# A decoder block's feed-forward part: gate and up projections by block products in Strassen's manner, the hidden values through DRAM

## The chip, the cores and the metric

One core of one Trainium2 chip runs the whole program in one launch. The metric is device time in microseconds (us), the median of three timed runs; a profiled execution beside them gives the trace. The engines that compute are TensorE (PE; its weight loads are listed as PEld), VectorE (DVE), ScalarE (ACT) and GpSimd (POOL). SyncE (SP) issues the DMAs; its queue is SPq.

## The reference

One decoder layer over 1024 tokens of width 1024, all float32: a norm and one combined input projection; eight heads of dilated sliding-window attention and eight heads of RWKV-7 time mixing; one output projection with a residual; then a norm and a SwiGLU feed-forward part of width 2816 (`D_FF`). The change lies in that last part:

```python
    x = x + mixed @ w_out
    xn2 = rms_norm(x, norm2_g).astype(x.dtype)
    ffn = (jax.nn.silu(xn2 @ w_gate) * (xn2 @ w_up)) @ w_down
    return x + ffn
```

## The kernel before, in words

**Precision.** A float32 product is made of three passes. Each operand is split (`split`): a rounded copy `hi` that ACT writes (fp32r) and a remainder `lo` that DVE or POOL forms as source minus `hi`. The passes are hi x hi, hi x lo and lo x hi, summed in PSUM (`passes`, `mm3`).

**Order of work.** The program is written as generators ("streams"), each with a rank. A planner (`Flow`) steps through them with modelled costs and times and emits every instruction in the order in which its model would start it; among those that are ready the lower rank goes first. `Wait`, `Mark`, `Get` and `Free` order the streams in the model and hand out PSUM banks. On the chip each engine then executes its own list strictly in that order, and waits at an instruction until the data it needs is there. SP issues its DMAs in order too.

**The feed-forward part.** It comes last, after attention, time mixing and the output projection (`outproj`, sums into `acc`, eight tiles of 128 tokens x 1024).
- `norms2` norms a tile of 128 tokens: ACT squares and sums, two small POOL steps give the factor, DVE multiplies by factor and gain (tile `nxn`), PE transposes eight blocks into two banks, and ACT and DVE split them into `x2h` and `x2l`. Two streams work on the first four tiles, then two on the last four. `xnh[h]`, `xnl[h]` hold token half h (512 tokens).
- `load_weights` brings 128 columns of gate or up (512 KB, unit u) into `ffraw`, ACT and DVE split them into `ffhi` and `fflo`. Units alternate gate, up, over 22 rows of 128 features (`NFF`).
- `ffproj` (PE): for each unit and token half 24 matmuls of 128x128 weights against 128x512 tokens: eight blocks of the inner dimension, three passes. The first two units are run on half 0 first, then on half 1.
- `hidden`: ACT takes the gate product from its bank through silu, DVE multiplies by the up product, ACT and DVE split the result into `hh` and `hl`, which stay in SBUF.
- `load_down` brings 128 rows of `w_down` and splits them; `down` takes two feature rows at a time (`GS`): for eight token tiles and two column halves six matmuls into one of two banks, 16 sums in all, and `accumulate` (DVE) adds each sum to `acc`. After the last group the tiles of `acc` are written out.

So projection and down projection alternate on PE, group by group. Eight PSUM banks are free in this part (`bank0` to `bank3`, `chain0`, `chain1`, `mm0`, `mm1`).

## Time and profile before

| | |
|---|---|
| timed runs | median 1536.94 us (1536.3 to 1537.02, three runs) |
| profiled execution | 1528.85 us, of it 1527.1 us span from the first to the last instruction |
| instructions in the trace | 23747 |
| DMA | 137.07 MB, mean 90 GB/s |
| HBM | 105.10 MB read, 26.21 MB written |
| chain that ended last | PE 57% of the span, DMA 3%, DVE 2% |

The page gives the busy time of each engine and its share of the span. PE's records of two neighbouring matmuls overlap (their ends are modelled), so the distance from start to start is what one costs. The chain is followed back from the last instruction, at each step to what released it. A group of instructions is one line: engine, operation, output<-inputs by the program's names, shapes, count, busy time, mean ns of one, idle time of the engine just before them and what ended it.

### The profile page before, as it was taken

How to read it: one execution, taken by the hardware profiler on the slowest of the kernel's cores; microseconds unless marked ns; L12 is line 12 of the kernel's file. 1: busy time of each engine (PE TensorE's matmuls, PEld its weight loads, DVE VectorE, ACT ScalarE, POOL GpSimd, SP SyncE). 2: the span in 40 equal slices, each digit the busy share in tenths (PEclk: the TensorE clock that was granted, in tenths of full speed). 3: DMA queues.
4: the chain of work that ended last, by engine and by line, in shares of the span. 5: the costliest groups of instructions: out<-in, count | busy, mean ns of one | idle time of the engine just before them, and what ended most of it. 6: DMA issues, size and time to landing. Idle time of an engine off the chain costs nothing.

```text
span 1527.1 us, 23747 instructions
## 1 busy us (share of the span) xinstructions
PE 1461.2 (96%) x8950; PEld 1181.5 (77%) x8950; DVE 774.6 (51%) x1705; ACT 610.3 (40%) x1546; POOL 340.5 (22%) x416
## 2 busy tenths in 40 slices
PE   8899999999899997998999999999999999999998
PEld 6667776776777776887878888888888888888887
DVE  5466677765664365776884424334242433424333
ACT  6434655557657765666754121111211112121110
POOL 5432434335544562325420000000000000000000
PEclk9999999999999998999999999999999999999999
DMA  6342232232323349995422021020211202021102
GB/s 203 104 113 67 62 99 69 76 89 77 105 83 107 106 141 283 276 229 146 112 70 85 27 69 56 29 69 14 83 36 47 59 25 77 21 70 55 42 1 111
DMA packets 171669, 137.07 MB, mean 90 GB/s; under 512 B 35617, under 2 KB 143393, under 8 KB 171554
## 3 DMA queue, kind: packets, MB, share of 16 engines
q1 hardware_dynamic: 171554, 135.55, 30.9%
q8 instruction: 71, 1.16, 0.3%
q14 instruction: 44, 0.36, 0.1%
HBM read 105.10 MB, written 26.21 MB: 86 GB/s over the span
## 4 chain that ended last, share of the span: by engine, by line
PE 57%; DMA 3%; DVE 2%; issue 1%; SPq 1%; ACT 1%; POOL 1%; POOLq 0%; ACTq 0%; DVEq 0%
PE bank L227 28%; PE chain L227 15%; PE mm L227 13%; DMA kk<-kl_d 1%; SPq L227 1%; DMA qv<-ql_d 0%; DMA kk<-kh_d 0%; DMA mixr<-mix_d 0%; DMA woraw<-in_w_out_dram 0%; ACT nxn L227 0%; DMA bias<-in_tab_dram 0%; DVE acc L227 0%; DVE ml L227 0%; ACT mh L227 0%; POOL nrs L227 0%
## 5 line engine op out<-in xcount | busy, mean ns | idle before, releaser
L227 ACT ACTIVATE dh<-wdraw 128x1024 fp32r<-128x1024 f32 x22 | 23.3, 1061 | 252.2 <-PE bank L227 229.1
L227 POOL TENSOR_TENSOR inlo<-inraw,inhi 128x512 fp32r<-128x512 f32 x62 | 81.6, 1320 | 110.3 <-ACT inhi L227 100.3
L227 DVE TENSOR_TENSOR acc<-chain,acc 128x512 f32<-128x512 f32 x96 | 66.4, 692 | 75.3 <-PE chain L227 75.3
L227 DVE TENSOR_TENSOR acc<-bank,acc 128x512 f32<-128x512 f32 x105 | 72.6, 691 | 62.2 <-PE bank L227 62.0
L227 DVE TENSOR_TENSOR fflo<-ffraw,ffhi 128x1024 fp32r<-128x1024 f32 x44 | 53.8, 1222 | 94.5 <-ACT ffhi L227 91.0
L227 ACT ACTIVATE hh<-sg 128x512 fp32r<-128x512 f32 x44 | 27.8, 633 | 152.9 <-DVE sg L227 152.9
L227 PE MATMUL bank<-x2l,ffhi 128*128 128x512 f32 x352 | 87.9, 389 | 0.0
L227 PE MATMUL bank<-x2h,fflo 128*128 128x512 f32 x352 | 87.5, 390 | 0.0
L227 PE MATMUL bank<-x2h,ffhi 128*128 128x512 f32 x352 | 87.1, 389 | 0.0
L227 ACT ACTIVATE ffhi<-ffraw 128x1024 fp32r<-128x1024 f32 x44 | 46.5, 1057 | 82.0 <-PE mm L227 52.9
L227 PEld LDWEIGHTS bank<-x2h,fflo 128*128 128x128 f32 x352 | 66.0, 188 | 13.8
L227 PEld LDWEIGHTS bank<-x2l,ffhi 128*128 128x128 f32 x352 | 66.1, 188 | 13.7
L227 PEld LDWEIGHTS bank<-x2h,ffhi 128*128 128x128 f32 x352 | 66.0, 188 | 13.7
L227 PE MATMUL chain<-dh,hh 128*128 128x512 f32 x176 | 68.6, 390 | 0.0
L227 PE MATMUL chain<-dl,hh 128*128 128x512 f32 x176 | 68.6, 390 | 0.0
L227 PE MATMUL chain<-dh,hl 128*128 128x512 f32 x176 | 68.5, 389 | 0.0
L227 PE MATMUL bank<-dh,hh 128*128 128x512 f32 x176 | 68.5, 389 | 0.0
L227 PE MATMUL bank<-dl,hh 128*128 128x512 f32 x176 | 68.5, 389 | 0.0
L227 PE MATMUL bank<-dh,hl 128*128 128x512 f32 x176 | 68.5, 389 | 0.0
L227 DVE TENSOR_TENSOR sg<-bank,sg 128x512 f32<-128x512 f32 x23 | 15.9, 692 | 83.0 <-PE bank L227 83.0
L227 DVE SCALAR_TENSOR_TENSOR S<-chain,ec,Sp 64x64 f32<-64x64 f32 x112 | 31.6, 282 | 51.0 <-PE chain L227 40.9
L227 PE MATMUL mm<-x2l,ffhi 128*128 128x512 f32 x224 | 55.3, 389 | 0.0
(359 smaller groups left out, 3692.9 us busy)
## 6 DMA issues: line engine op xcount, KB each, us to landing
inraw<-in_w_in_dram SPq DMA_DIRECT2D x62, 256.0 KB, 3.0
ffraw<-in_w_gate_dram SPq DMA_DIRECT2D x22, 512.0 KB, 4.7
ffraw<-in_w_up_dram SPq DMA_DIRECT2D x22, 512.0 KB, 4.9
wdraw<-in_w_down_dram SPq DMA_DIRECT2D x22, 512.0 KB, 3.5
rkv_d<-stage SPq DMA_DIRECT2D x24, 256.0 KB, 2.3
xt<-in_x_dram SPq DMA_DIRECT2D x8, 512.0 KB, 7.2
v_d<-v SPq DMA_DIRECT2D x16, 256.0 KB, 2.3
woraw<-in_w_out_dram SPq DMA_DIRECT2D x16, 256.0 KB, 4.9
```

The costliest lines, as they stand in the source:

```text
L227: op.fn(*op.a, **op.k)
```

## The change

For each feature row of 128 the gate and up weights are cut into four blocks: A11, A12 (gate, first and second half of the inner dimension), A21, A22 (up). The normed tokens are cut likewise: B11, B21 (tokens 0 to 511, both halves of the inner dimension), B12, B22 (tokens 512 to 1023). The four results, gate and up for both token halves, are made of seven block products in place of eight, in Winograd's form of Strassen's scheme: S1 = A21 + A22, S2 = S1 - A11, S3 = A11 - A21, S4 = A12 - S2, and on the token side T1 = B12 - B11, T2 = B22 - T1, T3 = B22 - B12, T4 = B21 - T2. A block product is 12 matmuls (four blocks, three passes).

- `norms2` now makes B11 and B21 of the first four tiles. `combine` norms the last four and forms B22 and T1 to T4 of them, each split in two.
- The first two feature rows (`NCL`) are made classically: four products K on the first token half, then four products L on T1 and B22, to which the partial sums kept from K are added. They use neither S nor T2 to T4.
- `fetch_ff` brings pieces of 256 KB into six raw buffers (`NFRAW`): four per feature row, later pieces of `w_down` and of h. `prepare_ff` forms S1 to S4 (POOL, DVE) and splits each operand into one of five buffers (`NOPS`); POOL makes the remainders of the unchanged blocks, DVE those of the sums.
- `ffproj` runs the products in the order P1, P6, P2, P7, P5, P4, P3. P2 adds onto P1's bank, P4 onto P7's, P3 onto P5's, each after another engine has read that bank: ACT copies P1 (`gates`), DVE forms U2 = P1 + P6, U3 = U2 + P7, C22 = U3 + P5, C21 = U2 + (P7 + P4), C12 = U2 + (P5 + P3) (`hidden`).
- The hidden values go to a DRAM tensor `h_d`, a block of 128 features x 512 tokens at a time.
- `down` starts when all products are done: for each token half eight banks collect the sums over all 22 feature rows; h and `w_down` are fetched and split again for it, `w_down` once per token half. `finals` adds each bank to `acc` once and writes it out in pieces of 256 KB.

```diff
-GS = 2
+NCL = 2
+NOPS = 5
+NFRAW = 6
...
+    h_d = dram.tile([DFF, S], F32, name="h_d")
...
-    def load_weights(pool, srcs, name, rbufs=1, sbufs=2, eng=DVE):
...
+    def combine(e):
+        for i in range(4 + e, 8, 2):
+            o = slice(128 * (i - 4), 128 * (i - 4) + 128)
+            yield Wait(("added", 1, i, 0), ("added", 1, i, 1), ("x2", 2 + e))
+            xn = T(pf, [128, D], F32, f"nxn{e}")
+            rs = T(pf, [128, 1], F32, f"nrs{e}")
+            yield from row_rsqrt(rs, T(pf, [128, 1], F32, f"nss{e}"), acc[i], xn)
+            yield DVE.scalar_tensor_tensor(out=xn, in0=acc[i], scalar=rs[:, 0:1], in1=g2bc, op0=ALU.mult, op1=ALU.mult)
+            tags = yield Get(n=2)
+            ps = [bank(t) for t in tags]
+            for q in range(2):
+                yield from transposes(ps[q], xn[:, 512 * q:512 * q + 512])
+            p12, p22 = [p.rearrange("p (k t) -> p k t", k=4) for p in ps]
+            (h11, l11), (h21, l21), (h22, l22) = [[t[:, :, o] for t in ff[x]] for x in ("B11", "B21", "B22")]
+            (h1, l1), (h2, l2), (h3, l3), (h4, l4) = [[t[:, :, o] for t in ff[x]] for x in ("T1", "T2", "T3", "T4")]
+            tt = T(pf, [128, 2, 4, 128], F32, f"tt{e}", tag=f"nxn{e}")
+            t1, t2 = tt[:, 0], tt[:, 1]
+            t3, t4 = T(pf, [128, 4, 128], F32, f"t3{e}", tag=f"sw{e + 1}"), t1
+            def less(o_, a_, b_, eng=DVE):
+                return eng.tensor_tensor(out=o_, in0=a_, in1=b_, op=ALU.subtract)
+            yield less(t1, p12, h11.bitcast(F32))
+            yield POOL.tensor_tensor(out=t1, in0=t1, in1=l11.bitcast(F32), op=ALU.subtract)
+            yield ACT.activation(h22, p22, AF.Copy)
+            yield ACT.activation(t3, p22, AF.Copy)
+            yield DVE.tensor_tensor(out=t3, in0=t3, in1=p12, op=ALU.subtract)
+            yield less(t2, p22, t1)
+            yield less(l22, p22, h22.bitcast(F32))
+            yield ACT.activation(h1, t1, AF.Copy)
+            yield ACT.activation(h3, t3, AF.Copy)
+            yield less(l1, t1, h1.bitcast(F32))
+            yield POOL.tensor_tensor(out=t4, in0=h21.bitcast(F32), in1=t2, op=ALU.subtract)
+            yield ACT.activation(h2, t2, AF.Copy)
+            yield DVE.tensor_tensor(out=t4, in0=t4, in1=l21.bitcast(F32), op=ALU.add)
+            yield less(l3, t3, h3.bitcast(F32), POOL)
+            yield less(l2, t2, h2.bitcast(F32))
+            yield ACT.activation(h4, t4, AF.Copy)
+            yield less(l4, t4, h4.bitcast(F32))
             yield Mark(("x2", i))
...
+    fraws, nop, fops = {}, [0], {}
+    corners = [(0, 0), (1, 0), (0, 1), (1, 1)]
+    pieces = [(p, r, q, "K") for p in range(NCL) for r, q in corners] + [(p, r, q, "L") for p in range(NCL) for r in range(2) for q in range(2)]
+    pieces += [(p, r, q, "S") for p in range(NCL, NFF) for r in range(2) for q in range(2)]
+    blocks2 = [(th, f, j, "down") for th in range(2) for f in range(NFF) for j in range(3)]
+    rawlist = pieces + blocks2
+    def fetch_ff():
+        for n, key in enumerate(rawlist):
+            if n >= NFRAW:
+                yield Wait(("rawfree", rawlist[n - NFRAW]))
+            raw = T(pf, [128, 4, 128], F32, "fraw", bufs=NFRAW)
+            if n < len(pieces):
+                p, r, q, _ = key
+                yield SP.dma_start(raw, wv[r][q][:, :, p * 128:(p + 1) * 128])
+            else:
+                th, f, j = key[0:3]
+                flat = raw.rearrange("p k t -> p (k t)")
+                if j == 1:
+                    yield Wait(("h", f, th))
+                    yield SP.dma_start(flat, h_d[f * 128:(f + 1) * 128, th * HB:(th + 1) * HB])
+                else:
+                    yield SP.dma_start(flat, w_down[f * 128:(f + 1) * 128, j // 2 * HB:j // 2 * HB + HB])
+            fraws[key] = raw
+            yield Mark(("raw", key))
+    def operand(key, src, eng):
+        n = nop[0]
+        nop[0] += 1
+        if n >= NOPS:
+            yield Wait(("opused", n - NOPS))
+        hi = T(pf, [128, 4, 128], F32R, "oph", bufs=NOPS)
+        lo = T(pf, [128, 4, 128], F32R, "opl", bufs=NOPS)
+        yield from split(src, hi, lo, eng)
+        fops[key] = hi, lo, n
+        yield Mark(("op", key))
+    def prepare_ff():
+        for key in pieces[0:8 * NCL]:
+            p, r, q, kind = key
+            yield Wait(("raw", key))
+            yield from operand((p, f"{kind}{r}{q}"), fraws[key], POOL)
+            yield Mark(("rawfree", key))
+        yield Wait(*[("x2", i) for i in range(4, 8)])
+        for p in range(NCL, NFF):
+            keys_ = [(p, r, q, "S") for r in range(2) for q in range(2)]
+            yield Wait(*[("raw", key) for key in keys_])
+            a11, a12, a21, a22 = [fraws[key] for key in keys_]
+            yield from operand((p, "A11"), a11, POOL)
+            s1 = fresh("sw1")
+            yield POOL.tensor_tensor(out=s1, in0=a21, in1=a22, op=ALU.add)
+            s2 = fresh("sw2")
+            yield DVE.tensor_tensor(out=s2, in0=s1, in1=a11, op=ALU.subtract)
+            yield from operand((p, "S2"), s2, DVE)
+            yield from operand((p, "A12"), a12, POOL)
+            s3 = fresh("sw3")
+            yield POOL.tensor_tensor(out=s3, in0=a11, in1=a21, op=ALU.subtract)
+            yield Mark(("rawfree", keys_[0]))
+            yield Mark(("rawfree", keys_[2]))
+            yield from operand((p, "S3"), s3, DVE)
+            yield from operand((p, "S1"), s1, DVE)
+            yield from operand((p, "A22"), a22, POOL)
+            yield Mark(("rawfree", keys_[3]))
+            s4 = fresh("sw4", "sw3")
+            yield DVE.tensor_tensor(out=s4, in0=a12, in1=s2, op=ALU.subtract)
+            yield Mark(("rawfree", keys_[1]))
+            yield from operand((p, "S4"), s4, DVE)
+        for key in blocks2:
+            yield Wait(("raw", key))
+            yield from operand(key, fraws[key], DVE)
+            yield Mark(("rawfree", key))
...
-    first = [flow.add(8.05, norms2(e, 2, 0, pf)) for e in range(2)]
-    flow.add(20, load_weights(pf, ffsrc, "ff", rbufs=2))
+    first = [flow.add(8.05, norms2(e)) for e in range(2)]
+    flow.add(20, fetch_ff())
+    flow.add(20.5, prepare_ff())
...
-    flow.add(8.05, norms2(0, 2, 1, pf))
-    flow.add(8.05, norms2(1, 2, 1, PG))
+    ff.update({x: [T(PG, [128, 4, HB], F32R, f"{x}{n}") for n in "hl"] for x in ("B22", "T1", "T2", "T3", "T4")})
+    for e in range(2):
+        flow.add(8.05, combine(e))
+    banks2 = {}
+    plan = [(p, f"{x}{j}") for x in "KL" for p in range(NCL) for j in range(1, 5)]
+    plan += [(p, x) for p in range(NCL, NFF) for x in ("P1", "P6", "P2", "P7", "P5", "P4", "P3")]
+    terms = {"K1": ("K00", "B11", "a", True, None), "K2": ("K10", "B11", "e", True, None), "K3": ("K01", "B21", "a", False, "s1"),
+             "K4": ("K11", "B21", "e", False, "q1"), "L1": ("L00", "T1", "d", True, None), "L2": ("L01", "B22", "d", False, None),
+             "L3": ("L10", "T1", "f", True, None), "L4": ("L11", "B22", "f", False, None),
+             "P1": ("A11", "B11", "a", True, None), "P2": ("A12", "B21", "a", False, "s1"), "P3": ("S4", "B22", "d", False, "C22"),
+             "P4": ("A22", "T4", "c", False, "u3"), "P5": ("S1", "T1", "d", True, None), "P6": ("S2", "T2", "b", True, None),
+             "P7": ("S3", "T3", "c", True, None)}
     def ffproj():
...
+        for p, x in plan:
+            w, b, acc_, begins, taken = terms[x]
+            yield Wait(("op", (p, w)), *[("x2", i) for i in (range(4) if b in ("B11", "B21") else range(4, 8))])
+            if taken:
+                yield Wait((taken, p))
+            if begins:
+                tag = yield Get()
+                banks2[p, acc_] = bank(tag), tag
+            ps = banks2[p, acc_][0]
+            wh, wl, n = fops[p, w]
+            i = 0
+            for a_, b_ in passes(wh, wl, *ff[b]):
+                for k in range(4):
+                    yield PE.matmul(out=ps, lhsT=a_[:, k, :], rhs=b_[:, k, :], start=(i == 0 and begins), stop=(i == 11), skip_group_check=True)
+                    i += 1
+            yield Mark(("opused", n))
+            yield Mark((x, p))
+    sg0, s1s, q1s = {}, {}, {}
+    def taken_(store, p, name):
+        store[p] = T(PG, [128, HB], F32, "first", bufs=4)
+        yield ACT.activation(store[p], banks2[p, name][0], AF.Copy)
+    def gates():
+        for p in range(NFF):
+            classical = p < NCL
+            yield Wait(("K1" if classical else "P1", p))
+            if not classical:
+                yield Wait(("h", NCL - 1, 1) if p < NCL + 4 else ("u2", p - 4))
+            yield from taken_(s1s, p, "a")
+            yield Mark(("s1", p))
...
+            yield Wait(("K3" if classical else "P2", p))
+            if p >= 2:
+                yield Wait(("h", p - 2, 0))
+            sg0[p] = T(PG, [128, HB], F32, "sg0", bufs=2)
+            yield ACT.activation(sg0[p], banks2[p, "a"][0], AF.Silu)
+            yield Free(banks2[p, "a"][1])
+            yield Mark(("sg0", p))
...
     def hidden():
...
+        def plus(o, p, name, other):
+            return DVE.tensor_tensor(out=o, in0=banks2[p, name][0], in1=other, op=ALU.add)
...
+        for p in range(NCL, NFF):
+            rows = slice(p * 128, (p + 1) * 128)
+            yield Wait(("P6", p), ("s1", p))
+            uu = T(pf, [128, 2, HB], F32, "uu", tag="nxn0")
+            u2, u3 = uu[:, 0, :], uu[:, 1, :]
+            yield plus(u2, p, "b", s1s[p])
+            yield Free(banks2[p, "b"][1])
+            yield Mark(("u2", p))
+            yield Wait(("P7", p))
+            yield plus(u3, p, "c", u2)
+            yield Mark(("u3", p))
+            yield Wait(("P5", p))
+            up1 = T(pf, [128, 2, HB], F32, "up1", tag="nxn1")
+            c22, c12 = up1[:, 0, :], up1[:, 1, :]
+            yield plus(c22, p, "d", u3)
+            yield Mark(("C22", p))
+            yield Wait(("P4", p), ("sg0", p))
+            c21 = T(pf, [128, HB], F32, "up0", tag="g2bc")
+            yield plus(c21, p, "c", u2)
+            yield Free(banks2[p, "c"][1])
+            yield POOL.tensor_tensor(out=c21, in0=c21, in1=sg0[p], op=ALU.mult)
+            yield SP.dma_start(h_d[rows, 0:HB], c21)
+            yield Mark(("h", p, 0))
+            yield Wait(("P3", p))
+            yield plus(c12, p, "d", u2)
+            yield Free(banks2[p, "d"][1])
+            yield ACT.activation(c12, c12, AF.Silu)
+            yield DVE.tensor_tensor(out=c22, in0=c22, in1=c12, op=ALU.mult)
+            yield SP.dma_start(h_d[rows, HB:S], c22)
+            yield Mark(("h", p, 1))
+    downs = {}
     def down():
...
+        yield Wait(("P3", NFF - 1))
+        for th in range(2):
+            for f in range(NFF):
+                d0, h, d1 = [(th, f, j, "down") for j in range(3)]
+                for hf, d in enumerate((d0, d1)):
+                    for i in range(4):
+                        if i == 0:
+                            yield Wait(("op", h), ("op", d))
+                        if f == 0:
+                            tag = yield Get()
+                            downs[th, i, hf] = bank(tag), tag
+                        m = 0
+                        for a_, b_ in passes(*fops[h][0:2], *fops[d][0:2]):
+                            yield PE.matmul(out=downs[th, i, hf][0], lhsT=a_[:, i, :], rhs=b_.rearrange("p k t -> p (k t)"),
+                                            start=(f == 0 and m == 0), stop=(f == NFF - 1 and m == 2), skip_group_check=True)
+                            m += 1
+                        if f == NFF - 1:
+                            yield Mark(("dsum", th, i, hf))
...
+    flow.run([flow.add(21, gates()), flow.add(22, hidden()), flow.add(22.5, finals()), flow.add(24, down()), flow.add(25, ffproj())])
```

## Rows read from the trace of the kernel before

**Rows 1.** The page, part 1: busy us, share of the span, instructions

```profile
PE 1461.2 (96%) x8950; PEld 1181.5 (77%) x8950; DVE 774.6 (51%) x1705; ACT 610.3 (40%) x1546; POOL 340.5 (22%) x416
```

**Rows 2.** Windows: engine busy us (count), clock, DMA share, GB/s

```profile
900.00:1000.00 100.00, 100.00 (x442) 82.76 (x441) 37.48 (x49) 15.18 (x19) 0.00 (x0) 1.00 0.13 37
```

**Rows 3.** PE's waits, 770 to 1527 us: total, times, longest; two of four

```profile
PE mm L227 <- DVE O L227: 1.1, 1, 1.1
...
PE bank L227 <- DVE d L227: 0.2, 1, 0.2
```

**Rows 4.** The chain of waits: start, us, what

```profile
891.36 5.44 PE bank L227 x24
```

**Rows 5.** Timeline at the part's start: start, us, what [idle before]

```profile
799.02 0.39 PE L227 MATMUL bank<-woh,ml 128*128 128x512 f32 x1
799.25 1.99 PE L227 MATMUL chain<-x2h,ffhi 128*128 128x512 f32 x8
...
799.27 0.19 ACT L227 ACTIVATION_READ_ACCUMULATOR nxn<-acc 128x1 f32 x1
799.36 1.05 ACT L227 ACTIVATE nxn<-acc 128x1024 f32<-128x1024 f32 x1
...
799.54 0.19 POOL L227 TENSOR_SCALAR nss<-nss 128x1 f32<-128x1 f32 x1 [5.81 <-ACT nxn L227]
799.82 0.54 POOL L227 TENSOR_TENSOR nrs<-nss,nhalf 128x1 f32<-128x1 f32 x1
...
800.39 1.28 DVE L227 SCALAR_TENSOR_TENSOR nxn<-acc,nrs,g2bc 128x1024 f32<-128x1024 f32 x1 [0.25 <-POOL nrs L227]
...
800.58 1.15 POOL L227 TENSOR_SCALAR nss<-nss 128x1 f32<-128x1 f32 x1 [0.23 <-ACT nxn L227]
...
802.39 1.28 DVE L227 SCALAR_TENSOR_TENSOR nxn<-acc,nrs,g2bc 128x1024 f32<-128x1024 f32 x1 [0.71 <-POOL nrs L227]
...
802.90 0.60 PE L227 MATMUL mm<-cs,nxn 128*128 128x128 f32 x4
803.25 0.94 PE L227 MATMUL chain<-x2h,fflo 128*128 128x512 f32 x3
```

**Rows 6.** Groups of instructions by form: busy us, mean ns

```profile
L227 ACT ACTIVATE hh<-sg 128x512 fp32r<-128x512 f32 x44 | 27.8, 633 | 152.9 <-DVE sg L227 152.9
...
L227 DVE TENSOR_TENSOR hl<-sg,hh 128x512 fp32r<-128x512 f32 x44 | 30.3, 689 | 16.1 <-ACT hh L227 16.1
...
L227 DVE TENSOR_TENSOR M<-bank,rc 128x512 f32<-128x512 f32 x16 | 11.1, 691 | 15.6 <-PE bank L227 15.5
...
L227 POOL TENSOR_TENSOR inlo<-inraw,inhi 128x512 fp32r<-128x512 f32 x62 | 81.6, 1320 | 110.3 <-ACT inhi L227 100.3 <-PE mm L227 6.3 <-PE chain L227 3.6
```

**Rows 7.** Timeline of DVE and POOL, 239 to 243 us

```profile
239.64 0.67 DVE L227 TENSOR_TENSOR ra<-kx,E 128x512 f32<-128x512 f32 x1
...
240.96 1.55 POOL L227 TENSOR_TENSOR inlo<-inraw,inhi 128x512 fp32r<-128x512 f32 x1 [6.09 <-ACT inhi L227]
241.28 1.78 DVE L227 TENSOR_TENSOR ra<-rx,E 128x512 f32<-128x512 f32 x1
```

**Rows 8.** Busy time by window after a starved stretch

```profile
700.00:702.00 2.00, 1.01 (x10) 0.80 (x9) 1.89 (x3) 1.17 (x4) 2.00 (x2) 1.00 0.35 121
702.00:704.00 2.00, 2.00 (x10) 1.99 (x11) 0.24 (x1) 1.32 (x6) 1.54 (x2) 0.50 0.77 230
704.00:706.00 2.00, 2.00 (x12) 1.66 (x11) 0.54 (x2) 1.57 (x4) 1.09 (x1) 0.65 0.93 253
```

**Rows 9.** The page, part 6: DMA issues, KB each, us to landing

```profile
inraw<-in_w_in_dram SPq DMA_DIRECT2D x62, 256.0 KB, 3.0
ffraw<-in_w_gate_dram SPq DMA_DIRECT2D x22, 512.0 KB, 4.7
```

**Rows 10.** PE's last instruction; busy time of the first 20 us

```profile
1522.84 0.39 PE L227 MATMUL bank<-dh,hl 128*128 128x512 f32 x1
...
0.00:20.00 20.00, 14.33 (x70) 8.21 (x71) 10.39 (x22) 11.90 (x23) 7.77 (x22) 1.00 0.89 310
```

More of the change, by code (lines that the diff above doesn't have):

```diff
@@ L1584, in accumulate @@
-    def accumulate():
-        m = 0
-        for g in range(NFF // GS):
-            for i in range(8):
-                for hf in range(2):
-                    cs_ = slice(hf * HB, (hf + 1) * HB)
-                    yield Wait(("dsum", m))
-                    yield DVE.tensor_tensor(out=acc[i][:, cs_], in0=products["down", m], in1=acc[i][:, cs_], op=ALU.add)
-                    yield Mark(("added", m))
-                    m += 1
-                    if g == NFF // GS - 1 and (hf or i == 7):
-                        cs_ = cs_ if i == 7 else slice(0, D)
-                        yield SP.dma_start(out[i * 128:(i + 1) * 128, cs_], acc[i][:, cs_])
```

131 lines of the change are left out of this document (49 added, 82 removed).

## The prediction

> **What bounds the kernel now.** I read the page's busy shares first: TensorE (PE) is busy 96% of the span, the next engine about half of it [rows 1]. A share over 1527.1 us mixes stages, so I cut the span into windows. From 800 us on, where the feed-forward part lies, a stretch of 100 us holds 100.00 us of PE at the full granted clock, while VectorE (DVE) has 37, ScalarE (ACT) 15, GpSimd (POOL) nothing and DMA an eighth [rows 2]. Then the waits of PE itself over 770 to 1527 us: the largest of four is 1.1 us, the sum 3.2 us [rows 3]. The chain of waits shows what one product costs: 24 matmuls in 5.44 us, 0.2267 us each, product after product without a gap [rows 4]. The part starts at 799.25 us, 0.23 us behind the last matmul of the output projection [rows 5], and ends near 1523 us [rows 10]. Count: 22 rows of 128 features, two projections, two token halves, 24 matmuls = 2112, and 22 x 16 x 3 = 1056 of the down projection; 3168 x 0.2267 = 718.1 us, which with the transposes fills that stretch. So PE alone bounds this half: a matmul taken away is worth 0.2267 us until something else ends last.
>
> **The change part by part.**
>
> *Matmuls.* The two classical rows keep 8 products of 12. Each of the 20 Strassen rows has 7 x 12 = 84 in place of 96: 240 fewer, of the same form (128x128 against 128x512, one weight load each). 240 x 0.2267 = **-54.4 us**. The down projection keeps its 1056.
>
> *Start.* The first product needs tokens 0 to 511 normed, as before, and that point is set by PE's own output projection [rows 5], so nothing is gained. DVE loses the two weight remainders it made there, POOL gets five of 1.32 us [rows 6], and a norm's small POOL steps can stand behind one. 0 to 1.3 us; I take **0.5**, since the wait is at most one operation and DVE is relieved.
>
> *The second token half.* Its four tiles now also yield T1 to T4, while PE has only the eight K products to do. Cover: 96 x 0.2267 = 21.8 us plus 32 transposes at 0.35 us for four (802.90 to 803.25) = 2.8 [rows 5], so K ends at 799.25 + 24.6 = 823.8. PE then needs T1 and B22 of all four tiles (T2 to T4 only later, behind 21.8 us of L products). Tiles go in pairs, since the buffer of a tile's normed rows is also that of its sums. Lower end, each step as soon as its inputs are there: from the square to the normed rows 4.3 us (799.36 to 802.39 + 1.28) [rows 5], transposes 1.0, then through T4 one after the other four DVE steps, two on POOL and an ACT copy: 4 x 0.69 + 2 x 1.32 + 0.63 and 0.9 of handovers (0.08 from 799.27 + 0.19 to 799.54 [rows 5]; I put 0.1 to 0.15 each) = 6.9 [rows 6]. Tile 5 has its normed rows at 803.67 and is through at 811.6; tile 7 then needs 4.3 + 1.0 + DVE 0.69, POOL 1.32, ACT 0.63, DVE 0.69 and 0.5 to have T1: 820.7, no stall. Upper end: POOL and DVE don't run independently. In this very place a POOL step of 0.19 us takes 1.15 while DVE works on two SBUF operands [rows 5], and a DVE operation of 0.67 us takes 1.78 beside a POOL one, ending after it [rows 7]. So I add both. Per tile: normed rows 1.28, four DVE steps with both operands in SBUF 2.76, small POOL steps 0.19 + 0.54 = 0.73, three POOL differences 3.96 = 8.7; two tiles 17.5; the other two up to T1 8.1; two more POOL steps of tile 6 2.6; six weight remainders of K and L that POOL makes meanwhile 7.9. Sum 36.1 us from 800.39: 836.5, a stall of 12.7. I take **9**, nearer the upper end, because rows 5 show the contention in the same instructions and place.
>
> The Trainium skill, page "SBUF — State Buffer", section "Who interferes with whom", says that a DVE instruction with two SBUF inputs and a GpSimd one that reads SBUF exclude each other for the whole instruction. The trace agrees (0.67 against 1.78 us). Taken strictly the rule gives the upper end here, and rival B below; without it the stall would be nil.
>
> *Clock.* After a stretch in which PE was half busy (1.01 of 2.00 us) the granted clock read 0.50 and 0.65 for two windows of 2 us [rows 8], the lower level of 1.2 GHz for most of them: 1.0 + 0.7 = 1.7 us. A stall of some us before L should cost this once: **2** (0 to 3).
>
> *One Strassen row.* PE: 84 x 0.2267 = 19.04 us. DVE: two differences, four remainders, five sums with PSUM, one product: 12 x 0.69 = 8.3. ACT: seven copies, the first sum, two silus: 10 x 0.63 = 6.3. POOL: three remainders, two sums, one product: 6 x 1.32 = 7.9. DMA: 1.5 MB per row. No engine is near 19. What can hurt is order. (a) P2 waits until ACT has taken P1 from the bank, P4 until DVE has added U3, P3 until DVE has added C22; all later products queue behind them on PE. Each has one other product, 2.72 us, between; 0.69 and a handover of 0.2 leave 1.8, more than the 1.11 that one exclusion costs [rows 7]; two in a row cost 0.4. (b) The fourth raw piece of a row is fetched only when S4 of the row before has been formed; from its landing to the next S4 stand 0.63 + 1.32 (A11), 1.32 (S1), 0.69 (S2), 0.63 + 0.63 + 1.32 (copies of S2 and A12, A12's remainder), 1.32 (S3), 0.63 and three DVE steps 2.07 = 10.6, handovers 1.4, and the fetch: 3.0 landing [rows 9] + 0.7: 15.7 us in all. With a landing like the feed-forward weights' now (4.7 [rows 9]) and three exclusions it is 20.7. As it stands it turns inside 19.04. Writes of h stand in SP's queue among the fetches, but only the last fetch of a row is urgent, and it is due some 10 us from either write. Bounds 0 to 16 (0.4 at two places, 20 rows, for (a)) or 20 x 1.7 = 33 for (b); I take **3**, by the sums that fit.
>
> *Down projection.* It runs behind all rows: per feature row and half three pieces of 256 KB in 24 x 0.2267 = 5.44 us, 145 GB/s, against 310 GB/s in the first 20 us [rows 10]; the 22 h blocks of each half go through DRAM, and w_down is read twice. ACT 3 x 0.63 and DVE 3 x 0.69 lie beside. A weight buffer is free a product group ahead and six raw buffers hold two feature rows, 10.9 us, against landings of 3 to 5. Cost 0, and 5 us if the last h blocks are waited for. 176 DVE sums into acc go, all beside PE: no gain, since PE waits for none.
>
> *End.* The last eight banks finish 0.68 us apart, not 1.36, so 2.1 MB go out in the last 5 us: at 310 GB/s 6.8 us. Now 4.3 us lie from the last matmul to the end of the span [rows 10]; I take **+0.5** (0 to 3).
>
> Sum: -54.4 + 0.5 + 9 + 2 + 3 + 0.5 = **-39.4 us**. The profiled execution took 1528.85 us (span 1527.1 and 1.75 around it), so 1489.5 by its own time. The three timed runs have a median of 1536.94, 8.1 more; I carry the difference over unchanged: **1497.5**.
>
> **The rivals.**
> A. All hidden: the K products cover the sums, no clock loss: 1536.9 - 54.4 + 1 = 1483.5. For it: the lower end above and three engines under half busy. Against it: rows 5.
> B. DVE and POOL exclude each other throughout: stall 12.7, clock 2, 16 us at the accumulating products, 1 at the ends: -54.4 + 31.7 = 1514. For it: rows 7. Against it: five of the 12 DVE steps per row take one operand from PSUM, and 16 such products in the stage where POOL works too have a mean of 0.691 us [rows 6].
> C. Slower: loop (b), fourth piece to S4 to fourth piece. PE follows the loop as soon as it is longer than 19.04; with 12 us lost elsewhere the gain is gone at 19.04 + 42.4 / 20 = 21.2. From 15.7 that takes a landing of 4.7 and four exclusions (15.7 + 1.7 + 4.4 = 21.8): 20 x 2.76 + 12 - 54.4 = +12.8, 1550. For it: every part is a seen duration. Against it: all worst cases at once, in every row.
> D. It doesn't save what it counts: matmuls leave, but the loop is near 21.2, so the time stays: 1537.
>
> **Chances.** Forecast 0.50, A 0.17, B 0.19, C 0.11, D 0.03. A measurement here tells about 0.2% (3 us) from no change. Faster 0.86, same 0.03, slower 0.11. Range: from just above A's time, 1484, to beyond B's with some of the loop, 1520; the forecast's own, 1489 to 1507.
>
> **What would show it.** PE records fall from 8950 to 8710; a Strassen row takes 19 to 19.4 us from P1 to P1, the granted clock full. One PE wait of 5 to 13 us stands about 815 to 835 us, before or inside K to L, released by DVE or ACT writing T1 or by the transposed rows. POOL is busy till the end of the rows, with DVE remainders of over 1 us beside it. PE is gapless in the down projection. I am wrong if rows take over 19.8 us (waits on C22, U3 or raw pieces), if the fetches of h stall PE, or if there is no stall before L.

## The result

The changed kernel takes 1496.67 us (median of four runs, 1491.3 to 1502.63) against 1536.98 us (1536.3 to 1538.71) for the kernel before: a ratio of 0.9737, 95% interval [0.9699, 0.9775], so 2.6% faster. In a later series the ratio was 0.9748 [0.9723, 0.9773]; one run of each kernel there (7811 and 2389 us) was slow and is left out of the medians and ratios of that series. The forecast was 1497.5. That it lies within 1 us of the first median is luck: the four runs behind this median spread over 11 us, and the median of the later series is 1493.39.

The first line of the changed kernel's page answers to [rows 1]: 240 matmuls fewer, PE's share hardly less, and three other engines with more to do.

```profile
PE 1420.0 (95%) x8710; PEld 1142.2 (76%) x8710; DVE 803.8 (54%) x1795; ACT 712.8 (47%) x1764; POOL 541.8 (36%) x564
```

I compare by places that can be found in every trace: K (the first product of the feed-forward part), L (the first product of the second token half), P1 (the first product of the first Strassen row), the first matmul of the down projection, and the end of the span. The changed kernel was profiled twice, the kernel before twice. Times are us behind K; K itself is given in us from the start of the span.

| | K at | L | P1 | down projection | end of span |
|---|---|---|---|---|---|
| before, two profiles | 799.25, 799.34 | | | | 727.8, 727.9 |
| changed, first profile | 813.39 | 32.0 | 59.9 | 444.2 | 687.4 |
| changed, second profile | 801.07 | 33.3 | 60.4 | 444.7 | 687.9 |

From K to the end the two kernels differ by 40 us, in either profile. Without a loss P1 would stand 24.6 + 21.8 = 46.4 behind K (the prediction's terms for K and L), so some 13.5 us are lost ahead of it. All of PE's waits from K to the end lie there; the waits of PE in the changed kernel from 812 to 1501 us (what waited, for whom: total, times, longest) are three. `T1h` and `T1l` are the rounded copy and the remainder of T1; `first` is ACT's copy of a K product out of its bank, without which the next product may not be added there:

```profile
PE bank L229 <- DVE T1l L229: 3.3, 1, 3.3
PE mm L229 <- ACT first L229: 3.0, 1, 3.0
PE bank L229 <- ACT T1h L229: 1.2, 1, 1.2
```

That is 7.5 us. More shows in windows of 2 us of the same stretch (columns as in [rows 2]; the clock is the third number from the end):

```profile
833.00:835.00 2.00, 0.00 (x0) 0.00 (x0) 1.90 (x4) 1.59 (x4) 1.64 (x3) 0.91 0.16 47
835.00:837.00 2.00, 1.91 (x5) 1.52 (x6) 1.99 (x1) 2.00 (x5) 1.75 (x2) 0.50 0.00 1
837.00:839.00 2.00, 2.00 (x12) 1.70 (x11) 1.29 (x1) 0.09 (x1) 1.83 (x3) 0.73 0.45 130
839.00:841.00 2.00, 2.00 (x14) 1.52 (x14) 1.60 (x2) 1.60 (x3) 0.32 (x1) 1.00 0.35 104
...
847.00:849.00 2.00, 0.00 (x0) 0.00 (x0) 2.00 (x3) 0.78 (x2) 2.00 (x2) 0.83 0.29 105
849.00:851.00 2.00, 1.08 (x3) 0.90 (x4) 2.00 (x3) 0.37 (x1) 1.37 (x2) 0.50 0.39 112
851.00:853.00 2.00, 2.00 (x6) 1.60 (x5) 2.00 (x2) 0.00 (x0) 2.00 (x2) 0.50 0.00 0
853.00:855.00 2.00, 2.00 (x6) 1.56 (x5) 1.91 (x3) 1.14 (x2) 0.28 (x1) 0.50 0.00 0
```

PE stands still, and the granted clock falls to its lower level (0.50, 1.2 GHz) and stays there for a while after PE is busy again: six matmul records in 2 us, where ten or eleven are usual. This happens twice. Busy time x (1 - clock), summed over the windows from K to P1, is what it costs: 4.1 us (4.6 in the second profile), an estimate from these rows. Waits 7.5, clock 4.1 and 0.65 for slower products (below) make 12.3 of the 13.5; 1.2 us I can't assign.

Who was late? DVE, ACT and POOL of the changed kernel just ahead of those waits (timeline: start, duration, what, in brackets the idle time before and its releaser), first DVE, then ACT, then POOL:

```profile
826.49 1.79 DVE L229 TENSOR_TENSOR tt<-tt,B21l 128x512 f32<-128x512 f32 x1
828.20 0.68 DVE L229 TENSOR_TENSOR sg<-bank,sg 128x512 f32<-128x512 f32 x1
...
829.91 1.77 DVE L229 TENSOR_TENSOR T4l<-tt,T4h 128x512 fp32r<-128x512 f32 x1
...
834.68 2.32 DVE L229 SCALAR_TENSOR_TENSOR nxn<-acc,nrs,g2bc 128x1024 f32<-128x1024 f32 x1
```

```profile
831.78 1.06 ACT L229 ACTIVATE nxn<-acc 128x1024 f32<-128x1024 f32 x1 [2.31 <-DVE T4l L229]
...
834.46 0.58 ACT L229 ACTIVATE first<-mm 128x512 f32<-128x512 f32 x1
```

```profile
827.68 1.76 POOL L229 TENSOR_TENSOR tt<-B21h,tt 128x512 f32<-128x512 f32 x1
829.39 1.75 POOL L229 TENSOR_TENSOR opl<-fraw,oph 128x512 fp32r<-128x512 f32 x1
```

Two things are to be seen. DVE steps with both operands in SBUF take 1.77 to 1.79 beside POOL's, the one with an operand in PSUM (sg) 0.68: the contention that the prediction took from [rows 7]. It isn't everywhere: of DVE's 42 steps of 128x512 between K and P1, 11 take over 0.8 us. And the square that begins the norm of tile 6 (ACT, 831.78) waits for T4l of tile 4 (829.91 + 1.77), 18.4 us behind K: the second pair of tiles begins when the first is through. Which of the two costs the time was the question for the experiments.

Behind P1 there is no wait at all. A Strassen row takes (1257.58 - 873.31) / 20 = 19.21 us where 84 x 0.2267 is 19.04. The timeline of PE shows the difference inside the products (three lines of four matmuls each make one product):

```profile
1241.15 1.08 PE L229 MATMUL bank<-T2h,oph 128*128 128x512 f32 x4
1242.08 1.07 PE L229 MATMUL bank<-T2l,oph 128*128 128x512 f32 x4
1242.98 1.07 PE L229 MATMUL bank<-T2h,opl 128*128 128x512 f32 x4
1243.89 1.09 PE L229 MATMUL bank<-B21h,oph 128*128 128x512 f32 x4
1244.81 1.10 PE L229 MATMUL bank<-B21l,oph 128*128 128x512 f32 x4
1245.75 1.10 PE L229 MATMUL bank<-B21h,opl 128*128 128x512 f32 x4
1246.68 1.08 PE L229 MATMUL mm<-T3h,oph 128*128 128x512 f32 x4
```

The product on B21 takes 2.79 us (1243.89 to 1246.68; 0.93 to 0.94 from one line to the next), the others 2.72 to 2.74. All products on B11 and B21 are like this, two in each row, and all of K. The down projection has no gap: 443 matmuls in 100 us (442 in [rows 2]).

```profile
1300.00:1400.00 100.00, 100.00 (x443) 82.84 (x442) 40.70 (x63) 33.18 (x56) 0.00 (x0) 1.00 0.49 166
```

### The profile page after: what moved, and what is told of

Read it like the earlier page. It is cut to its first block, busy times and chain, and to the rows that moved or that the text cites. A ratio compares the mean times of both kernels' runs of the same rounds, so it can differ in the third digit from the quotient of the medians.

```text
span 1500.8 us, 24737 instructions
## 1 busy us (share of the span) xinstructions
PE 1420.0 (95%) x8710; PEld 1142.2 (76%) x8710; DVE 803.8 (54%) x1795; ACT 712.8 (47%) x1764; POOL 541.8 (36%) x564
## 4 chain that ended last, share of the span: by engine, by line
PE 54%; DMA 4%; DVE 3%; SPq 1%; ACT 1%; issue 1%; POOL 0%; ACTq 0%; POOLq 0%; DVEq 0%
PE bank L229 26%; PE mm L229 15%; PE chain L229 13%; DMA kk<-kl_d 2%; SPq L229 1%; DMA bias<-in_tab_dram 1%; DMA qv<-qh_d 1%; DVE acc L229 1%; DMA acc<-in_x_dram 0%; DMA mixr<-mix_d 0%; DVE tt L229 0%; DVE ml L229 0%; DVE T1l L229 0%; DVE nxn L229 0%; POOL ro L229 0%
## 5 line engine op out<-in xcount | busy, mean ns | idle before, releaser
L229 ACT ACTIVATE oph<-fraw 128x512 fp32r<-128x512 f32 x208 | 126.6, 628 | 223.4 <-PE bank L229 117.6
L229 POOL TENSOR_TENSOR opl<-fraw,oph 128x512 fp32r<-128x512 f32 x76 | 101.4, 1336 | 210.6 <-PE bank L229 110.2
L229 DVE TENSOR_TENSOR opl<-fraw,oph 128x512 fp32r<-128x512 f32 x132 | 87.7, 689 | 143.3 <-ACT oph L229 143.3
L229 ACT ACTIVATE oph<-sw 128x512 fp32r<-128x512 f32 x80 | 50.6, 632 | 178.0 <-DVE sw L229 71.9
L229 PE MATMUL bank<-oph 128*128 128x512 f32 x176 | 68.5, 389 | 0.0
L229 PE MATMUL bank<-opl,oph 128*128 128x512 f32 x176 | 68.5, 389 | 0.0
L229 PE MATMUL bank<-oph,opl 128*128 128x512 f32 x176 | 68.5, 389 | 0.0
L229 DVE TENSOR_TENSOR opl<-sw,oph 128x512 fp32r<-128x512 f32 x80 | 56.0, 701 | 18.7 <-ACT oph L229 18.7
L229 ACT ACTIVATE Ub<-chain 64x64 f32<-64x64 f32 x128 | 28.2, 220 | 56.7 <-DVE VS L229 54.9
L229 POOL TENSOR_TENSOR sw<-fraw 128x512 f32<-128x512 f32 x40 | 51.9, 1298 | 0.0
L229 ACT ACTIVATE inhi<-inraw 128x512 fp32r<-128x512 f32 x62 | 38.7, 624 | 14.9 <-PE mm L229 7.0
L229 PE MATMUL chain<-Rb,M 128*128 128x128 f32 x128 | 27.8, 299 | 11.7 <-DVE Rb L229 11.5
```

What stands on the lines that cost most here:

```text
L229: op.fn(*op.a, **op.k)
```

## The experiments

K stood at 801 to 814 us in the twelve profiles of the changed kernel and its variants, with nearly the same instructions ahead of it. A variant's total from one execution therefore says little; the distances from K repeat within 1.3 us (L) and 0.5 us (P1 and down projection), as the two rows of the changed kernel show, and I judge by these. Each variant was profiled once, so a difference between variants no larger than that says nothing.

| edit | K at | L | P1 | down projection |
|---|---|---|---|---|
| changed kernel | 813.39 | 32.0 | 59.9 | 444.2 |
| one classical row | 805.08 | 29.0 | 45.5 (one row fewer ahead) | 448.9 |
| bank copies first | 806.78 | 35.1 | 63.4 | 447.6 |
| T2 to T4 split later | 806.74 | 28.2 | 50.0 | 442.6 |
| POOL reads added | 806.27 | 43.0 | 69.9 | 454.2 |
| POOL writes added | 804.83 | 41.8 | 67.3 | 451.6 |
| sums in PSUM | 802.90 | 35.4 | 60.0 | 444.2 |
| second norms early | 808.06 | 32.0 | 54.4 | 438.6 |
| both of these | 808.19 | 32.7 | 56.8 | 441.0 |
| same residue | 810.26 | 31.9 | 59.8 | 440.6 |
| early norms + same residue | 814.03 | 32.0 | 54.4 | 435.1 |

**Less cover: one classical row.**

```diff
-NCL = 2
+NCL = 1
```

> One classical row in place of two, so 21 Strassen rows: 12 matmuls fewer, and K, which covers the sums of the second token half, has 48 matmuls in place of 96 (11 us less cover); L likewise. Theory (the sums set the start of L, K only fills the time): L still starts 29 to 33 us behind the first product, PE waits 11 us more there, the seven products of the added row come on top, so the feed-forward part ends 5 to 9 us later than in the changed kernel. Rival (the sums are slowed by K's own remainders and copies): L starts 24 to 27 us behind, and the part ends within 2 us of the changed kernel's.

L starts 29.0 us behind K, the low end of the theory's range: with 11 us less of K work it comes 3.0 us earlier, and PE's waits ahead of P1 grow from 7.5 to 13.5 us. So mainly the sums set that point, and K fills the time. The down projection comes 4.7 us later, although 12 matmuls (2.7 us) are gone; the theory's 5 to 9 was a little high.

**Order of the queues: bank copies first.** gates() gets rank 8.0 in place of 21.

> Only the order in which the engines' queues are filled: the steps that take products out of the banks stand ahead of the sums of the second token half instead of behind them. Theory (the amount of DVE and POOL work up to T1 sets the start of L): PE no longer waits 3.0 us for ACT's first copy of a K product, but waits that much longer for T1: L starts 31 to 33 us behind K as before, total within 1 us. Rival (that copy, queued behind the norm's square and the split of T4 on ACT, is a wait of its own): L starts 28 to 30 us behind K, and the end comes 3 to 4 us earlier.

Neither: the wait for ACT's copy vanishes, but the norms and T1 come later (PE waits 2.1 and 1.7 us for nxn, 3.3 for T1h, 2.7 for T1l), L 35.1 behind K, 3.4 us lost by the down projection. The 3.0 us on `first` were a symptom of the same late sums; put ahead of them, the copies delay them.

**Work moved behind the start of L.** The edit, shortened; its comments stand for lines left out.

```diff
 # combine: only B22 and T1; raw T2, T3 stored
+    def combine_later():   # rank 20.2: splits of T2, T3; T4 and its split
...
+    *([("x2b", i) for i in range(4, 8)] if b in ("T2", "T3", "T4") else [])
```

> Only the sums of the second token half change place: before L only B22 and T1 are formed; T2 and T3 are left as raw sums, and their splits and the whole of T4 are made later, while the L products run. In the changed kernel K starts 32.0 us before L and 59.9 us before P1 of row 2, and PE waits 3.0 us for ACT's first copy, 1.2 and 3.3 us for T1 of tile 7. Theory (DVE and POOL taking turns through the sums of four tiles set the start of L): a third of the POOL and DVE steps leave that stretch, so K to L falls to 26 us (24 to 28), the windows there show no clock below 0.9, and K to P1 of row 2 falls to 49 us (47 to 52). With a wait of up to 2 us at P4 or P6 of row 2 if the late splits are too late. Rival (the chain of one tile, norm to transposes to T1, sets it, not the amount of work): L starts 31 to 32 us behind K as before. Rival (the work only moves, and what was late before L is late behind it): K to L falls, but the first products of row 2 wait as much, and K to P1 stays 58 to 60.

L comes 3.8 us earlier (28.2 behind K, just over the theory's 28), P1 9.9 earlier, as the theory had it, and then most is given back inside row 2. The edit also takes the sums out of the buffer of the normed rows: the squares of tiles 6 and 7 begin 8.6 and 11.7 us behind K, in the changed kernel 18.4 and 21.5. So the 9.9 us belong to both, less work ahead of L and an earlier second pair. The largest sum of PE's waits behind K in this run, and the ACT timeline at the longest wait, show where:

```profile
PE chain L229 <- ACT first L229: 7.7, 2, 6.7
```

```profile
868.02 0.63 ACT L229 ACTIVATE oph<-sw 128x512 fp32r<-128x512 f32 x1 [3.26 <-DVE sw L229]
868.56 0.58 ACT L229 ACTIVATE first<-chain 128x512 f32<-128x512 f32 x1
```

The copy that frees P1's bank stands behind weight copies that wait for DVE, which wait for what the late splits held up. The third product waits 6.7 us: part (a) of the prediction's row, which had priced it at 0.4. The clock falls during that wait and costs 1.45 us more. Of 9.9 us gained, 1.6 are left at the down projection: the work had mostly moved.

**What POOL's time costs: added reads, added writes.** Per tile, ahead of T2:

```diff
+            for _ in range(2):
+                yield POOL.tensor_tensor(out=pad, in0=pad, in1=pad, op=ALU.subtract)
```

and in the other kernel four `POOL.memset(pad, 0.0)` in their place. `pad` is a dead tile.

> Work is only added: per tile of the second half two more POOL steps that read SBUF (a dead tile minus itself, 1.27 us each alone), put ahead of T2. Theory (POOL's SBUF reads and DVE's two-operand steps take turns, so POOL's time is DVE's time too): eight such steps, at 1.3 to 1.75 us, of which seven or eight lie ahead of T1 of tile 7: L starts 8 to 12 us later than in the changed kernel, 40 to 44 behind K; DVE's two-operand steps stay at 1.7 to 1.8. Rival (POOL has slack there): under 4 us later.

> Work is only added: in the same places per tile four POOL steps that write a dead tile and read nothing, about 0.5 us each, so that POOL's queue is held about as long as by the two reading steps. Theory (what hurts is POOL reading SBUF beside DVE, not its queue): DVE's two-operand steps beside these take 0.69, and L starts 1 to 5 us later than in the changed kernel, clearly less than with the reading steps. Rival (POOL's queue is the bound): the same 8 to 12 us as with the reading steps.

The eight reads took 10.0 us of POOL and put L 11.0 and the down projection 10.0 later. The sixteen writes took 9.1 us of POOL's queue (0.52 us each, 0.57 from one start to the next) and put them 9.8 and 7.4 later: that is the rival of the second expectation. DVE isn't slowed by the writes: beside seven of them on POOL (first fence) a step with both operands in SBUF takes 0.69 us (second fence).

```profile
813.07 4.03 POOL L229 MEMSET sw<- 128x512 f32 x7
```

```profile
816.30 0.69 DVE L229 TENSOR_TENSOR T1l<-tt,T1h 128x512 fp32r<-128x512 f32 x1 [0.87 <-ACT T1h L229]
```

So POOL's queue is itself in the chain ahead of P1: added work there comes out as 0.8 to 1.0 us for each us at the down projection, whether it blocks DVE or not. The Trainium skill, page "SBUF — State Buffer", section "Who interferes with whom", says that DVE's two-SBUF instructions contend with GpSimd's reads, not with its writes; these durations agree (0.69 beside writes, 1.77 beside reads). It does not follow that the contention is what sets the end.

**Without the contention: T1 and T2 summed in PSUM.** The same 8 DVE and 3 POOL steps per tile, one ACT copy more, and each DVE step has one operand in PSUM.

```diff
-            t1, t2 = tt[:, 0], tt[:, 1]
+            t1, t2 = p12, p22          # the banks of the transposed rows
...
-            yield POOL.tensor_tensor(out=t1, in0=t1, in1=l11.bitcast(F32), op=ALU.subtract)
+            yield DVE.tensor_tensor(out=t1, in0=t1, in1=l11.bitcast(F32), op=ALU.subtract)
```

> The same sums for the second token half by nearly the same steps per tile (8 on DVE and 3 on POOL as before, one ACT copy more), but T1 and T2 are summed in the banks that hold the transposed rows, so that each of the 8 DVE steps has one operand in PSUM, where the changed kernel has 4 of 8 with both in SBUF. Theory (POOL and DVE exclude each other when both read SBUF, and that stretches these sums): DVE steps here take 0.69 us beside POOL's, POOL's 1.3; DVE's own work up to T1 of tile 7 is 3 x 8 x 0.69 + 4 x 1.28 + 2.8 + 1.4 = 26 us, so L starts 26 to 29 us behind K (32.0 in the changed kernel), and P1 of row 2 is 51 to 56 behind K (59.9). Rival (number of steps and their order): K to L 31 us or more, DVE steps are no faster, or the longer hold of the banks stalls PE.

The contention is gone: of DVE's 42 steps of 128x512 between K and P1 one takes over 0.8 us (11 in the changed kernel), their sum falls from 37.5 to 29.3 us. And in this order of steps it is worth nothing: L is later (35.4, outside the theory's 26 to 29), P1 stands at 60.0, the down projection at 444.2. DVE's timeline shows what became of the time: it is through with the first pair at 820.6 and then idle, with two slow norm steps, until the second pair's rows are transposed at 830.5. ACT's line is the square of the last tile: it waits for the first pair's T4l, which is now POOL's step, and begins 20.6 us behind K (21.5 in the changed kernel).

```profile
819.91 0.69 DVE L229 TENSOR_TENSOR T2l<-bank,T2h 128x512 fp32r<-128x512 f32 x1 [0.76 <-ACT T2h L229]
824.03 2.31 DVE L229 SCALAR_TENSOR_TENSOR nxn<-acc,nrs,g2bc 128x1024 f32<-128x1024 f32 x1 [3.42 <-POOL nrs L229]
828.28 2.28 DVE L229 SCALAR_TENSOR_TENSOR nxn<-acc,nrs,g2bc 128x1024 f32<-128x1024 f32 x1 [1.95 <-POOL nrs L229]
830.48 0.68 DVE L229 TENSOR_TENSOR t<-t,mm 128x512 f32<-128x512 f32 x1
```

```profile
823.52 1.06 ACT L229 ACTIVATE nxn<-acc 128x1024 f32<-128x1024 f32 x1 [1.34 <-POOL T4l L229]
```

PE now waits once for 5.6 us (T1h) and once for 2.5 (nxn), 8.1 in all, and loses 3.7 us to the clock: no less than the changed kernel.

**Without the series of the norms: the second pair's norms early.** Tiles 6 and 7 are normed and transposed while 4 and 5 are summed; the sums stay in SBUF, in other buffers. Three more things change with it, which the excerpt below does not show: the sums of tiles 6 and 7 still come behind those of 4 and 5, but within a tile T1 is now split before T3 is formed, and there are five raw buffers in place of six.

```diff
-        flow.add(8.05, combine(e))                     # for e in 0, 1: tiles 4+e, 6+e in turn
+        flow.add(8.05, combine(i))                     # for i in 4 to 7
...
-            t1, t2 = tt[:, 0], tt[:, 1]                # in the buffer of the normed rows
+            t1 = T(pf, [128, 4, 128], F32, f"ta{e}", tag=f"sw{e + 1}")
+            t2 = T(pf, [128, 4, 128], F32, f"tb{e}", tag="sw3" if e else "sw4")
```

> The norms of tiles 6 and 7 no longer wait for the sums of tiles 4 and 5: the sums leave the buffer of the normed rows (T1, then the raw T3, then T4 in one buffer, T2 in another; one raw weight buffer fewer, 5 for 6), and each tile has a stream of its own in the planner. All sums stay in SBUF, steps per engine as in the changed kernel. Theory (two reasons together: the pair of tiles in series leaves DVE and POOL idle while the second pair is normed, and DVE and POOL stretch each other): the gap goes, the stretching stays: L starts 28 to 31 us behind K (32.0), T4l of the first pair and the norm of the second no longer follow each other. Rival (the stretching alone sets it, as the sum of both engines' times that I took before): 32 to 36. Rival (the series alone): 25 to 27.5.

> Both: norms of tiles 6 and 7 early, as in the run beside it (six raw buffers kept), and T1 and T2 summed in PSUM, so that no DVE step of the sums has both operands in SBUF. With the sums in PSUM alone, DVE's steps were 0.68 us and POOL's 1.30, but L started 35.4 us behind K, since DVE stood idle from 820.6 to 830.5 us while the second pair was normed and transposed. Theory (series and stretching are the two reasons): DVE's own steps are the bound, 30 x 0.69 + 4 x 1.28 = 26 us from 1 us behind K: L starts 26 to 29 us behind K, P1 of row 2 50 to 54 (59.9), and the stretch from K to the down projection falls from 444.2 to 436 to 440. Rival (something else, such as ACT's queue or the hold of the banks): 31 or more.

By L, the point that I had named, the first looks like a failure: 32.0, the rival's number. By P1 and the down projection it gains 5.5 and 5.6 us. L begins when PE has done K, and K still holds 3.1 us of waits and the fall of the clock; but little is late behind it (0.8 and 0.2 us). The squares of tiles 6 and 7 start at 812.86 and 814.39 (4.8 and 6.3 us behind K, not 18.4), and PE's waits behind K are short (three of five):

```profile
PE bank L229 <- ACT first L229: 1.9, 1, 1.9
PE bank L229 <- ACT T1h L229: 0.8, 1, 0.8
PE chain L229 <- DVE nxn L229: 0.6, 1, 0.6
```

The clock falls once, at a cost of 1.6 us in place of 4.1. P1 stands at 54.4, still 8.0 behind the 46.4 without a loss. The run with both edits has DVE at 0.69 again, misses all three of its ranges and gains less, 3.2 us: PE waits once for 6.5 us (clock 2.2), for T1h of tile 7, which stands on ACT behind T4h of tile 6, and that behind POOL. Whether a better order would make the PSUM sums pay is open; it wasn't tried.

**Where the 3% in B11 and B21 comes from.** By the kernel's own allocation these two blocks began at 992 modulo 2048 bytes (the residue), the split weights, T1 to T4 and B22 at 1120. In the kernel before, the moving blocks and the weights of a product shared a residue (992 in the projections, 1184 in the down projection), and a matmul took 0.2267. Four small tiles placed ahead of B11 bring it to 1120 as well.

```diff
+    for e in range(2):
+        T(pf, [128, 1], F32, f"nrs{e}"), T(pf, [128, 1], F32, f"nss{e}")
     ff = {x: [T(pf, [128, 4, HB], F32R, f"{x}{n}") for n in "hl"] for x in ("B11", "B21")}
```

> Only addresses change: four small tiles are placed ahead of B11 and B21, so that these two begin at the same residue modulo 2048 bytes as the split weights and the blocks T1 to T4 and B22. In the changed kernel a product on B11 or B21 takes 2.79 us (0.2335 a matmul) and one on the other blocks 2.72 (0.2267). Theory (the residue of the moving operand against the weights sets that 3 per cent): all products take 2.72, a Strassen row falls from 19.21 to 19.05 us, K by 0.6, and the stretch from K to the down projection by some 3.5 to 4 us. Rival (it is the place in memory, or what the other engines read and write at that time): B11 and B21 stay at 2.79 and rows at 19.2.

The theory, to the number: the same product in this run takes 2.72 us, a row (1250.87 - 870.07) / 20 = 19.04, and the down projection comes 3.6 us earlier.

```profile
1237.27 1.07 PE L229 MATMUL bank<-B21h,oph 128*128 128x512 f32 x4
1238.18 1.07 PE L229 MATMUL bank<-B21l,oph 128*128 128x512 f32 x4
1239.08 1.07 PE L229 MATMUL bank<-B21h,opl 128*128 128x512 f32 x4
1239.99 1.07 PE L229 MATMUL mm<-T3h,oph 128*128 128x512 f32 x4
```

K got shorter too, but P1 did not move (59.8): what sets P1 is the sums, so K's share of the gain was swallowed by the waits.

**The part ahead of K, and the two edits together.**

> The kernel before once more, for where its feed-forward part starts. In its first profile it started at 799.25 us; with the changed kernel and four variants whose instructions up to there are the same it was 813.39, 806.74, 810.26, 805.08 and 806.78. Theory (the part ahead varies from run to run by some us and the change does nothing there): start at 800 to 812, and from start to the end of the span 727 to 729 us as in the first profile. Rival (the change makes the part ahead later): start at 798 to 801 again.

> The changed kernel once more, on the chip and beside the runs of the kernel before that the version above uses. Theory (the part ahead of K varies from run to run, what follows does not): K starts between 803 and 814 us, K to L 32.0, K to P1 of row 2 59.9 and K to the down projection 444.2, each within 0.3 us of the first profile; the median 1488 to 1500, 2.4 to 2.9 per cent under the kernel before. Rival (the stall ahead of row 2 is itself a matter of chance): K to P1 of row 2 differs by over 1 us.

> The two edits that shortened the feed-forward part, together: norms of tiles 6 and 7 early (438.6 us from K to the down projection in place of 444.2) and the blocks B11 and B21 at the weights' residue (440.6). Theory (they are independent: one concerns the gap ahead of row 2, the other the time of each product on B11 and B21): 444.2 - 5.6 - 3.6 = 435.0 us from K to the down projection (434 to 436.5), all products 2.72 us, P1 of row 2 about 53.5 behind K, and the time 7 to 11 us under the changed kernel's beside it. Rival (a shorter K leaves less cover for the sums, so part of one gain eats the other): 436.5 to 438.6.

The kernel before started its feed-forward part at 799.34 again (outside the theory's 800 by a hair, inside the rival's 798 to 801), the changed kernel at 801.07 in its second profile and at up to 814.03 in variants: the part ahead varies by 13 us among these, and the change itself need account for no more of it than the 1.7 us of the closest pair. The second profile lies below the 803 to 814 expected, and its distances differ from the first by 1.3 us (L) and 0.5 (P1, down projection), more than the 0.3 expected; but the stall came again, with the same three waits, so it is no matter of chance.

The traces show in part where the 12.3 us between the two profiles of the same program come from. After 250 of the 5750 matmuls ahead of K the first profile is 6.1 us behind the second (63.7 and 57.6 us), and in their first 100 us the granted clock differs, first the first profile, then the second:

```profile
0.00:100.00 100.00, 90.10 (x445) 66.04 (x446) 51.28 (x97) 47.49 (x84) 44.89 (x68) 0.91 0.44 137
```

```profile
0.00:100.00 100.00, 87.14 (x462) 64.06 (x463) 56.77 (x105) 50.54 (x88) 47.24 (x70) 1.00 0.47 148
```

Most of the rest comes in two steps between 590 and 730 us; why, was not followed up. The kernel before varies as well, from 1528.41 to 1538.71 us over both series, and both its profiles (1528.85 and 1528.98) lie at the short end.

The gains of the two edits add: 444.2 - 5.6 - 3.6 = 435.0 expected, 435.1 measured. In time the combined version has a ratio to the kernel before of 0.9711 [0.9685, 0.9737], the changed kernel in the same series 0.9748 [0.9723, 0.9773]: medians 1489.53 and 1493.39, 3.9 us apart and not the 7 to 11 expected, with a part ahead of K that varies by more than that, and the two intervals overlap. The 9 us are shown between K and the down projection, in one profile; the totals don't contradict them, and don't measure them. That profile gives a granted clock of 0.95 in gapless stretches, where the others give 1.00, with as many matmuls (443 from 900 to 1000 us, as in the run with the same residue alone), so I compare its distances as they are.

## Why the prediction was right, step by step

- *Matmuls*, -54.4: the records fell by exactly 240, at the same 0.2267 us but for the products on B11 and B21 (below).
- *Start*, +0.5 (0 to 1.3): mis-sized. Both profiles of the changed kernel have two PE waits for nxn shortly ahead of K, of 1.2 and 0.6 to 0.7 us, where the kernel before has one of 0.2; K is 1.7 us later in the closest pair. The prediction allowed for one operation.
- *The second token half* and *clock*, 9 + 2: 13.5 us in all. The waits were 7.5, less than the 9. Of them 4.5 are on T1, as named; 3.0 are on ACT's copy `first`, ahead of the second pair's transposes, which the prediction did not have. Its sign, one wait of 5 to 13 us at 815 to 835 us, did not come: there are three, the longest 3.3 us, from 832 to 850 us. The clock was mis-sized: 4.1 and 4.6 us, not 2. I had it fall once; it came back in between and fell a second time, 1.5 and 2.6 us in the first profile. The upper estimate, tile 7's T1l at 37.25 us behind K, was right to the us (848.11 + 1.75 = 849.86, 36.5 behind), but that is partly luck. I added POOL's and DVE's times because they exclude each other, 24 of the 36.1 us being POOL's; they do exclude each other, but up to P1 this stretched DVE's steps by only some 8.5 us (37.5 less 42 x 0.69). Taking the exclusion away gave nothing, while the two edits that let the second pair begin earlier moved P1 by 9.9 us (T2 to T4 later) and 5.5 (early norms). The buffer shared by a tile's normed rows and its sums was in my text, as a detail of the lower estimate; with the order of the sums it weighed more than the exclusion. How the 13.5 us divide between these is not shown, since each edit also changed the order of steps.
- *One Strassen row*, 3: 20 x 0.17 = 3.4 us. The size was right by luck and the reason wrong. Not one wait stands in a row, at (a) or at (b); the loss is the products on B11 and B21, a term that the prediction did not have. The run with T2 to T4 split later shows that (a) was a real danger: 6.7 us in one place as soon as ACT's queue is late.
- *Down projection*, 0: right, gapless, with POOL idle and DMA at half.
- *End*, +0.5: the last matmul starts at 1496.71, 4.1 us from the end of the span, against 4.3 [rows 10]: -0.2.
- The terms measured, -54.4 + 13.5 + 3.4 - 0.2 = -37.7, and some 2.6 us that the kernel before had in this part (727.8 less 718.1 for 3168 matmuls, 2.8 for the transposes and 4.3 at the end; a wait of 0.6 for nxn is in it, the rest I can't assign) make the 40 us. With the start, +1.7, that is some -38.6 against the forecast of -39.4: it came out by errors that cancel, the clock and the start too small, the 2.6 us left out. That is luck, as is the step from there to the timed 1497.5: the 8.1 us between profile and timed median, which I carried over, did not come back with the change (its profiled executions took 1502.63 and 1490.84, with medians of 1496.67 and 1493.39).

Rival A (1483.5) needed the sums to be hidden behind K; they were not, by 13.5 us at P1. Rival B (1514) needed the exclusion at every accumulating product; none stalled, and of the 80 DVE remainders of S1 to S4 in the rows one took over 1 us, though the prediction expected them beside POOL. Rival C needed four exclusions and a landing of 4.7 us in each row; the raw pieces of w_gate and w_up landed in 3.7 and 3.0 us (medians) and PE never waited for one.

## What to carry to other kernels

When sums must be ready for the bounding engine, look first for a buffer or a loop that puts their rounds in series, and only then for contention between the engines that form them: here DVE's steps could be made 22% shorter in sum for no gain, and with the norms early as well the two edits gained less (3.2 us) than the early norms alone (5.6). Judge such an edit at a point behind all that it may delay (the down projection, not the first product): moving work gained 9.9 us at one point and gave 8.3 back at the next. And count PE's stops as well as their length: a fall of the clock with such a stop cost another 1.45 to 6.0 us here, and no stop under 1 us brought one.

## What the hardware showed that I had not expected

- A product whose moving operand began 128 bytes off the weights' residue modulo 2048 took 2.79 us in place of 2.72, 0.2335 us a matmul against 0.2267; with addresses alone changed it was 2.72, and two blocks that share a residue of 992 cost 0.2267 in the kernel before. Which residue matters (2048 or a smaller power), and whether PE's reads or another engine's are behind it, was not tried.
- POOL steps that only write (0.52 us each) left a DVE step with both operands in SBUF at 0.69 us; POOL steps that read SBUF stretched such steps to as much as 1.79.
- What a fall of the clock cost did not follow the length of the stop that brought it: 1.6 us with one of 1.9 (early norms), 2.2 with one of 6.5 (both edits), 1.45 with one of 6.7 (T2 to T4 later). It cost more where PE stopped again before the clock was back: 3.7 with stops of 2.5 and 5.6 us (sums in PSUM), 4.8 with 10.8, 3.5 and 1.3 (POOL reads), 6.0 with 8.9, 2.8 and 1.4 (one classical row).
